# A two-layer hybrid block in split fp32: rotary projections and five gates turned, attention in steps, a last half chunk in two banks

## The chip, the cores and the metric

The kernel runs on one core of one Trainium2 chip. TensorE (PE) multiplies, VectorE (DVE), ScalarE (ACT) and GpSimd (POOL) work on what lies in SBUF and PSUM, SyncE (SP) starts transfers. The metric is device microseconds of one execution. The kernel before takes 939.03 us, the median of three runs (938.96 to 939.28).

## The reference, cut to what matters

Two layers over 256 tokens with 2048 channels, each of the form x + mix(norm(x) @ w_in) @ w_out. The even layer holds retention (8 heads, q and k rotated) and a selected attention of 8 heads; the odd layer a convolution over the sequence and an attention at three dilations. Every mixed part is multiplied by a gate, the silu of a projection of its own:

```python
def even_layer(x, ...):
    h = rms_norm(x, norm_g) @ w_in
    rq, rk, rv, rz, nq, kc, vc, ks, vs, kw, vw, ng, nz = split_cols(h, EVEN_SPLITS)
    o = retention_chunkwise(rotary(heads(rq), pos), rotary(heads(rk), pos), heads(rv))
    a_out = merge(rms_norm(o, ret_g)) * silu(rz)
    b_out = nsa_attention(nq, kc, vc, ks, vs, kw, vw, ng, ...) * silu(nz)
    return x + concat([a_out, b_out]) @ w_out

def odd_layer(x, ...):
    cu, cg, cz, dq, dk, dv, dz = split_cols(rms_norm(x, norm_g) @ w_in, ODD_SPLITS)
    c_out = conformer_conv(cu, cg, ...) * silu(cz)      # 1024 wide
    d_out = dilated_attention(dq, dk, dv, ...) * silu(dz)   # 512 wide
    return x + concat([c_out, d_out]) @ w_out
```

## The kernel before

All the large products are made in three passes of a short fp32 format (fp32r). A weight piece of 512 KB (`raw`, 128 rows x two k x 512 columns) is fetched by SP; ACT casts it to `wh` (line 109) and DVE subtracts, `wl = raw - wh` (line 110). The inputs are split likewise into `xh` and `xl`, one block of 512 channels each. A projection of 512 columns goes over four blocks (chunks) of channels, two pieces each. It has two forms in `project`:

- The normal form (lines 145 to 147): 128 tokens are the stationary operand and 512 weight columns stream. Tokens stand in the partitions of the result; two banks `mm0`, `mm1` of PSUM hold the two halves of the tokens.
- The flipped form (lines 139 to 141), used for the four rotary projections: 128 weight columns are stationary, 256 tokens stream, three products. Columns stand in the partitions, so that a head is turned as rotary needs it.

The gates are projected in the normal form: ACT takes them from PSUM with silu and the token's factor (line 708). Three in the odd layer and two in the even layer multiply a result that has channels in the partitions, so PE first transposes `z` in 8 pieces of 128x128 (`gated`, `turn`, line 315).

The weight pieces have five buffers (tag `raw`, `wh`, `wl`), and the projections three banks of PSUM (tag `mm`), which go round: the third projection half after a given one takes its bank. Two more banks hold scores (`sc`), two serve transposes (`tr`), one holds sums (`o`).

The order of instructions on each engine is not written out by hand. A scheduler with a simulated timeline sets it from the order in the code and from priorities (`tc.high_priority(offset=HPO)`); work of the attention is handed in as `pieces`, placed behind given weight chunks through `extra`/`take`. Every engine then runs its own list in order and waits at semaphores.

Names in the stages that matter here. Even layer: `pcs`, `pc`, `pch`/`pcl` are compressed scores and their split, `pst` (line 538) holds copies of them, `p`, `sm`, `nm` belong to a head's softmax (line 560 makes its maximum), `pTh`/`pTl` are its turned split. `rot` and `rT` are the rotated parts of q or k (lines 640 to 644), `rrow` (line 235) the row of token factors, `pb` the constants it is multiplied into. Odd layer: `acc` is the convolution's result, `chsum`/`csq`/`lnm`/`lnr`/`lnrow` its normalisation, `dsc`, `dp`, `dnm`, `dpT`, `dpo`, `do` the dilated attention's scores, weights, factors, turned weights, sums and results. `ACT_TABLE_LOAD` comes where ACT goes from one kind of function to another (silu, exp, square root).

At the start two projections share the first input blocks (`project_both`, lines 272 to 274: `mm` and `both`), and the squares of each block for its norm are taken behind the block's first projection (`square_block`, `sqb`, `sqs`). At the end the last half of the last projection is added to `xtok` in two parts of 256 columns (line 965), each with its own transfer to the output.

## Time and profile before

| | |
|---|---|
| profiled execution, whole | 939.11 us |
| its span, first to last instruction | 937.3 us |
| granted TensorE clock, mean | 0.999 |
| PE busy | 930.5 us (99%), 4949 matmuls |
| DVE busy | 642.3 us (69%) |
| ACT busy | 507.5 us (54%) |
| POOL busy | 71.1 us (8%) |
| DMA | 173.48 MB, mean 185 GB/s |

The profiled execution takes 1.8 us more than its span, and lies 0.08 us above the median of the runs. Busy time of PE is made of modelled ends, so that matmuls overlap in the rows; what one costs is read from the distance of the starts. Idle time of an engine matters only where PE waits for it.

### The profile page before, as it was taken

What the parts mean: (1) busy time and instruction counts of PE and PEld (TensorE: products, weight loads), DVE (VectorE), ACT (ScalarE), POOL (GpSimd) and SP (SyncE); (2) the same over time, 40 slices, a digit from 0 to 9 for tenths busy, and PEclk for the clock granted to TensorE, in tenths of its full rate; (3) what the DMA queues carried; (4) which work ended last, traced back from release to release, by engine and by line L of the source; (5) the groups of instructions that cost most, each with busy time, mean ns of one, the idle gap of its engine ahead of it and who ended that gap; (6) DMA issues with size and microseconds to landing.
All of it is one profiled execution on the core that took longest, in us unless ns stands there. A gap on an engine that the chain in (4) does not pass through costs nothing.

```text
span 937.3 us, 13151 instructions
## 1 busy us (share of the span) xinstructions
PE 930.5 (99%) x4949; PEld 798.7 (85%) x4949; DVE 642.3 (69%) x947; ACT 507.5 (54%) x762; POOL 71.1 (8%) x72
## 2 busy tenths in 40 slices
PE   8999999999999999999999999999999999999998
PEld 7889989989998888888888888888888888888886
DVE  7687657875654564654464499999999998546552
ACT  7566656655544544544465353556665444797341
POOL 0111100320220100000000000000000002200000
PEclk9999999999999999999999999999999999999999
DMA  9967754354446555555555555555555656434461
GB/s 332 348 204 220 249 189 149 120 176 156 152 164 207 161 170 182 185 195 181 196 185 168 192 180 180 190 190 190 185 186 185 202 197 189 148 116 157 149 226 53
DMA packets 52512, 173.48 MB, mean 185 GB/s; under 512 B 5728, under 2 KB 10720, under 8 KB 52320
## 3 DMA queue, kind: packets, MB, share of 16 engines
q1 hardware_dynamic: 52304, 172.63, 55.8%
q8 instruction: 39, 0.64, 0.3%
q14 instruction: 25, 0.20, 0.1%
q10 hardware_dynamic: 144, 0.01, 0.0%
HBM read 170.52 MB, written 2.10 MB: 184 GB/s over the span
## 4 chain that ended last, share of the span: by engine, by line
PE 97%; DMA 1%; DVE 1%; ACT 0%; issue 0%; SPq 0%; DVEq 0%
PE mm L145 25%; PE mm L147 25%; PE mm L146 25%; PE mm L139 3%; PE mm L141 3%; PE mm L140 3%; PE tr L315 3%; DMA raw<-in_ew 1%; PE dpo L931 1%; PE dsc L911 1%; PE cmph L377 1%; PE tr L579 1%; PE both L273 1%; PE both L274 0%; PE both L272 0%; PE mm L274 0%
## 5 line engine op out<-in xcount | busy, mean ns | idle before, releaser
L110 DVE TENSOR_TENSOR wl<-raw,wh 128x1024 fp32r<-128x1024 f32 (+2 forms) x322 | 385.1, 1202 | 215.0 <-ACT wh L109 208.1
L109 ACT CAST wh<-raw 128x1024 fp32r<-128x1024 f32 (+2 forms) x322 | 328.4, 1025 | 343.5 <-PE mm L147 252.1
L146 PE MATMUL mm<-wl,xh 128*128 128x512 f32 (+1 forms) x1056 | 406.4, 385 | 0.0
L145 PE MATMUL mm<-wh,xh 128*128 128x512 f32 (+1 forms) x1056 | 406.1, 386 | 0.0
L147 PE MATMUL mm<-wh,xl 128*128 128x512 f32 (+1 forms) x1056 | 403.3, 384 | 0.0
L147 PEld LDWEIGHTS mm<-wh,xl 128*128 128x128 f32 x1056 | 198.4, 188 | 38.1
L145 PEld LDWEIGHTS mm<-wh,xh 128*128 128x128 f32 x1056 | 198.2, 188 | 37.9 <-issue 0.2
L146 PEld LDWEIGHTS mm<-wl,xh 128*128 128x128 f32 x1056 | 198.5, 188 | 37.4
L801 DVE SCALAR_TENSOR_TENSOR cps<-apad,pb,cps 128x256 f32<-128x256 f32 x240 | 116.8, 487 | 5.3
L139 PE MATMUL mm<-xh,wh 128*128 128x256 f32 x256 | 73.2, 287 | 0.0
L140 PE MATMUL mm<-xh,wl 128*128 128x256 f32 x256 | 72.8, 285 | 0.0
L141 PE MATMUL mm<-xl,wh 128*128 128x256 f32 x256 | 72.5, 283 | 0.0
L140 PEld LDWEIGHTS mm<-xh,wl 128*128 128x128 f32 x256 | 49.0, 192 | 0.0
L141 PEld LDWEIGHTS mm<-xl,wh 128*128 128x128 f32 x256 | 49.0, 191 | 0.0
L139 PEld LDWEIGHTS mm<-xh,wh 128*128 128x128 f32 x256 | 48.9, 191 | 0.0
L567 ACT ACTIVATE p<-p,nm 128x128 f32<-128x128 f32 (+1 forms) x32 | 14.2, 445 | 15.5 <-DVE nm L563 15.4
L643 POOL TENSOR_TENSOR rot<-rot,pb 128x512 f32<-128x512 f32 x8 | 11.2, 1406 | 78.3 <-ACT rot L641 78.0
L299 ACT ACTIVATE sq<-d 128x128 f32<-128x128 f32 x48 | 14.3, 303 | 0.3
L273 PE MATMUL both<-wl,xh 128*128 128x512 f32 x32 | 12.8, 401 | 1.2 <-DVE wl L110 1.2
L644 POOL TENSOR_TENSOR rT<-rT,rot 128x512 f32<-128x512 f32 x8 | 13.1, 1660 | 0.0
L272 PE MATMUL both<-wh,xh 128*128 128x512 f32 x32 | 12.6, 394 | 0.0
L274 PE MATMUL both<-wh,xl 128*128 128x512 f32 x32 | 12.5, 390 | 0.0
(294 smaller groups left out, 724.0 us busy)
## 6 DMA issues: line engine op xcount, KB each, us to landing
raw<-in_ow SPq DMA_DIRECT2D x128, 512.0 KB, 4.5
raw<-in_ew SPq DMA_DIRECT2D x110, 512.0 KB, 4.2
raw<-in_ewo SPq DMA_DIRECT2D x32, 512.0 KB, 4.0
raw<-in_owo SPq DMA_DIRECT2D x24, 512.0 KB, 4.1
raw<-in_ewn SPq DMA_DIRECT2D x16, 268.0 KB, 3.5
xtok<-in_xtok SPq DMA_DIRECT2D x1, 2048.0 KB, 8.3
raw<-in_w1k SPq DMA_DIRECT2D x4, 512.0 KB, 6.4
raw<-in_w1v SPq DMA_DIRECT2D x4, 512.0 KB, 4.2
```

Source lines behind the costliest of these rows:

```text
L109: nc.scalar.copy(wh[:, k, :n], r)
L110: nc.vector.tensor_sub(wl[:, k, :n], r, wh[:, k, :n].bitcast(F32))
L139: nc.tensor.matmul(o, wh[:, k, cs], xh[:, kk, :], start=first and j == 0, stop=False, **kw)
L140: nc.tensor.matmul(o, wl[:, k, cs], xh[:, kk, :], start=False, stop=False, **kw)
L141: nc.tensor.matmul(o, wh[:, k, cs], xl[:, kk, :], start=False, stop=last, **kw)
L145: nc.tensor.matmul(o, xh[:, kk, ts], wh[:, k, :n], start=first, stop=False)
L146: nc.tensor.matmul(o, xh[:, kk, ts], wl[:, k, :n], start=False, stop=False)
L147: nc.tensor.matmul(o, xl[:, kk, ts], wh[:, k, :n], start=False, stop=last)
L273: nc.tensor.matmul(o, xh[:, kk, ts], wl[:, k, :], start=False, stop=False)
L299: nc.scalar.activation(sqv[:, t, h, :], view[:, t, h, :], AF.Square, accum_out=ss[:, t * nh + h:t * nh + h + 1])
L315: nc.tensor.transpose(pt[:, i * 128:(i + 1) * 128], b, ident)
L801: nc.vector.scalar_tensor_tensor(p, src, w, p, op0=ALU.mult, op1=ALU.add)
```

## The change

- The rotary projections and five gates (two even, three odd) go through `project_turned`: blocks of 256 columns, 128 weight columns stationary. `xh` and `xl` of a block now lie in one tile `xx`, so that one product of `wh` with both (2x256 columns streamed) and one of `wl` with `xh` (256 columns) take the place of three. The result stands in two halves of the bank, which are added on the way out.
- `evac_rotary` works per head: ACT copies one half to `rx` (two buffers), DVE adds the other, ACT makes two rotated copies, DVE and POOL multiply and add as before.
- A turned gate leaves PSUM by an ACT copy, a DVE add, a DVE product with the row of token factors (`rrow`, and a new `rrow2` for the odd layer) and a silu on ACT, for each 128 columns. Its transposes go; the product with the result is a plain DVE product (`done`).
- The pieces of the selected attention are cut into scores, turning and sums, ten in all; those of retention into scores and sums.
- The squares of the first three input blocks wait for the second projection's last piece of that block (`late`).
- The last half chunk of the last projection goes into two banks: 12 products of 256 columns in place of 6 of 512; the first 256 columns leave together with the sum so far of the other 256.
- `pst` is filled by 12 copies of 512 columns in place of 24 of 256.

```diff
+EV_TURNED = [(512 * h + 1024 * i + 256 * j, 512 * h + 1024 * i + 256 * j + 256)
+             for h in range(2) for i in range(2) for j in range(2)]
+EV_TURNED += [(6680 + 256 * j, 6936 + 256 * j) for j in range(4)]
...
+    def project_turned(src, lhs, evac, extra=None):
+        nch = src.shape[0]
+        acc = [ps.tile([128, 512], F32, name=f"mm{t}", tag="mm", bufs=MMB) for t in range(2)]
+        for c in range(nch):
+            with tc.high_priority(offset=HPO):
+                raw, wh, wl = (wp.tile([128, 2, 512], d, name=n, tag=n).rearrange("p a (b n) -> p (a b) n", n=256)
+                               for n, d in (("raw", F32), ("wh", F32R), ("wl", F32R)))
+                nc.sync.dma_start(raw, src[c])
+                nc.scalar.copy(wh, raw)
+                nc.vector.tensor_sub(wl, raw, wh.bitcast(F32))
+            xh, _, both = lhs[c]
+            for t in range(2):
+                cs = slice(t * 128, t * 128 + 128)
+                for k in range(4):
+                    last = c == nch - 1 and k == 3
+                    kw = dict(skip_group_check=True)
+                    nc.tensor.matmul(acc[t], wh[:, k, cs], both[:, :, k, :], start=c == 0 and k == 0, stop=False, **kw)
+                    nc.tensor.matmul(acc[t][:, :S], wl[:, k, cs], xh[:, k, :], start=False, stop=last, **kw)
+                if last:
+                    with tc.high_priority(offset=HPO):
+                        evac(t, acc[t])
...
+                    if tail and t == 1 and c == nch - 1 and hf == 1:
+                        end = ps.tile([128, 512], F32, name="mm2", tag="mm", bufs=MMB)
+                        for j, o in enumerate((acc[t][:, :256], end[:, :256])):
+                            js = slice(256 * j, 256 * j + 256)
+                            for k in range(2):
+                                kk, kw = 2 * hf + k, dict(skip_group_check=True)
+                                nc.tensor.matmul(o, xh[:, kk, ts], wh[:, k, js], start=j == 1 and k == 0, stop=j == 0, **kw)
+                                nc.tensor.matmul(o, xh[:, kk, ts], wl[:, k, js], start=False, stop=j == 0, **kw)
+                                nc.tensor.matmul(o, xl[:, kk, ts], wh[:, k, js], start=False, stop=j == 0 or k == 1, **kw)
+                            with tc.high_priority(offset=HPO):
+                                tail(j, acc[t], end)
+                        continue
...
+    def square_block(b, after=None):
         if b == 0:
             sqs[0] = hp.tile([128, S], F32, name="sqs", tag="h")
         sq = hp.tile([128, 4, S], F32, name="sqb", tag="h")
-        nc.scalar.activation(sq, xT[:, 4 * b:4 * b + 4, :], AF.Square)
+        nc.scalar.activation(sq, xT[:, 4 * b:4 * b + 4, :], AF.Square, bias=0.0 if after is None else after)
         nc.vector.tensor_add(sq[:, 0:2, :], sq[:, 0:2, :], sq[:, 2:4, :])
...
-                if q == 0 and c < nch - 1:
-                    square_block(c)
+                if q == 1 and c < nch - 1:
+                    nc.gpsimd.tensor_copy(late[:, c:c + 1], parts[1][1][:, 1, 511:512].bitcast(F32))
+                    nc.gpsimd.memset(late[:, c:c + 1], 0.0)
+                    square_block(c, late[:, c:c + 1])
...
-    pst = [hp.tile([128, 4, 2, 128], F32R, name=f"pst{g}", tag="h") for g in range(2)]
-    for h in range(8):
-        g, r = h // 4, slice(32 * (h % 4), 32 * (h % 4) + 32)
+    pst = [hp.tile([128, 2, 4, 128], F32R, name=f"pst{g}", tag="h") for g in range(2)]
+    for j in range(4):
         for n, src in enumerate((pch, pch, pcl)):
-            v = src[r].rearrange("p (t g) k -> p t g k", t=2)[:, :, g, :]
-            (nc.vector.tensor_copy if n else nc.scalar.copy)(pst[g][32 * n:32 * n + 32, h % 4], v)
+            (nc.vector.tensor_copy if n else nc.scalar.copy)(pst[j // 2][32 * n:32 * n + 32, j % 2], src[32 * j:32 * j + 32])
...
+    def nsa_piece(m):
+            if m > 2 and m % 2:
+                nsa_sum(m - 2)
+            if 0 < m < 9:
+                if m % 2:
+                    for n in ("h", "l"):
+                        npt[n] = pp.tile([128, 6, 2, 128], F32R, name="pT" + n, tag="pT")
+                nsa_turn(m - 1, nsp.pop(m - 1), npt["h"], npt["l"])
+            if m < 8:
+                nsp[m] = nsa_scores(m)
+    pieces = [nsa_piece(m) for m in range(10)]
...
-        def f(b, p):
-            hs = slice(2 * b, 2 * b + 2)
-            pv = p.rearrange("p (h s) -> p h s", h=2)
-            cb, sb = (x.unsqueeze(1).to_broadcast([128, 2, S]) for x in (cosR, sinR))
-            nc.scalar.copy(rot[0:64, hs, :], pv[64:128])
-            nc.scalar.copy(rot[64:128, hs, :], pv[0:64])
-            nc.vector.tensor_tensor(T[:, hs, :], pv, cb, op=ALU.mult)
-            nc.gpsimd.tensor_tensor(rot[:, hs, :], rot[:, hs, :], sb, op=ALU.mult)
-            nc.gpsimd.tensor_add(T[:, hs, :], T[:, hs, :], rot[:, hs, :])
+        def f(h, p):
+            x = sp.tile([128, S], F32, name="rx", tag="rx", bufs=2)
+            nc.scalar.copy(x, p[:, S:])
+            nc.vector.tensor_add(x, p[:, :S], x)
+            nc.scalar.copy(rot[0:64, h, :], x[64:128])
+            nc.scalar.copy(rot[64:128, h, :], x[0:64])
+            nc.vector.tensor_mul(T[:, h, :], x, cosR)
+            nc.gpsimd.tensor_mul(rot[:, h, :], rot[:, h, :], sinR)
+            nc.gpsimd.tensor_add(T[:, h, :], T[:, h, :], rot[:, h, :])
...
-            project(ew[4 + 3 * hf + i], 512, lhs, evac_rotary(T), extra=take((1,3)), flip=True)
+            f = evac_rotary(T)
+            for j in range(2):
+                project_turned(a["ewt"][4 * hf + 2 * i + j], lhs, lambda t, p: f(2 * j + t, p), extra=take((3,)))
...
-        pieces += [ret_piece(hf, h, qk[0], qk[1], v, dm, gr, hold) for h in range(4)]
...
+        pieces += [together(pieces.pop(), scores[0]) if hf else scores[0]]
+        pieces += [together(sums[h - 1], scores[h]) for h in range(1, 4)] + [sums[3]]
...
-        project(src, 512, lhs, lambda t, p: nc.scalar.activation(z[:, t, :], p, AF.Silu, scale=r[:, t:t + 1]),
-                extra=extra)
-
-        def turn():
-                pt = transpose4([z[:, t, (2 * j + k) * 128:(2 * j + k + 1) * 128] for k in range(2) for t in range(2)])
-                with tc.high_priority(offset=HPO):
-                    d = dst[:, hs, :].rearrange("p a b -> p (a b)")
-                    nc.vector.tensor_mul(d, pt, d)
-                    split(xh[:, hs, :], xl[:, hs, :], dst[:, hs, :])
...
+    def gated(srcs, dst, row, turn, n=4):
+        z = hp.tile([128, 4, S], F32, name="z", tag="h")
+        xh, xl, xx = block_pair()
+        for j in range(2):
+            def evac(t, p, j=j):
+                v = z[:, 2 * j + t, :]
+                nc.scalar.copy(v, p[:, S:])
+                nc.vector.tensor_add(v, p[:, :S], v)
+                nc.vector.tensor_mul(v, v, row)
+                nc.scalar.activation(v, v, AF.Silu)
+            project_turned(srcs[j], lhs, evac, extra=first(turn if j == 0 else None, take((1, 3))))
+        def done():
+                nc.vector.tensor_mul(dst[:, hs, :], dst[:, hs, :], z[:, hs, :])
+                split(xh[:, hs, :], xl[:, hs, :], dst[:, hs, :])
...
+    rrow2 = token_row(rstd2, "rrow2")
...
-        extra = take(range(4))
-        if i == 2:
-            extra = {c: extra.get(c, []) + ([turns[c]] if c < 2 else []) for c in range(4)}
-        block, turn = gated(ow[13 + i], (acc[0], acc[1], do)[i], rstd2, extra)
+        turn = (lambda: [f() for f in turns]) if i == 2 else None
+        block, done = gated(a["owt"][2 * i:2 * i + 2], (acc[0], acc[1], do)[i], rrow2, turn)
         mix.append(block)
-        turns.append(turn)
+        turns.append(done)
...
-            w = 256 if n == 3 and t else 512
-            for c in range(0, 512, w):
-                k = 512 * n + c
-                v = xtok[:, t, k:k + w]
-                nc.vector.tensor_add(v, p[:, c:c + w], v)
-                nc.sync.dma_start(out[t, :, k:k + w], v)
+            v = xtok[:, t, 512 * n:512 * n + 512]
+            nc.vector.tensor_add(v, p, v)
+            nc.sync.dma_start(out[t, :, 512 * n:512 * n + 512], v)
         return f
+    def evac_tail(j, p, end):
+        v = xtok[:, 1, D - 512:]
+        if j == 0:
+            nc.vector.tensor_add(v, p, v)
+            nc.sync.dma_start(out[1, :, D - 512:D - 256], v[:, :256])
+        else:
+            nc.vector.tensor_add(v[:, 256:], end[:, :256], v[:, 256:])
+            nc.sync.dma_start(out[1, :, D - 256:], v[:, 256:])
```

How the order changes is seen best at three places.

VectorE in the even layer, where the compressed scores have been split and the first rotary projection leaves PSUM; before, the two halves of the projection (`mm0_1567`, `mm1_1568`) are read by the product for `rT`:

```order
L538 COPY pst0_1530<-pcl_1522 32x256 x4
L538 COPY pst1_1531<-pcl_1522 32x256 x4
L560 ISA p_1867,nm_1866<-sc_1859,pm_518 128x2x128
L560 ISA nm_1866 128x1
L560 ISA p_1867,nm_1866<-sc_1859,pm_518 128x128
L560 ISA nm_1866 128x1
L560 ISA p_1867,nm_1866<-sc_1859,pm_518 128x2x128
L560 ISA nm_1866 128x1
L110 TENSOR_TENSOR wl_2083<-raw_2081,wh_2082 128x1024
L460 TENSOR_TENSOR pTl_1691<-tr_1717,pTh_1690 128x4x128
L563 TENSOR_SCALAR nm_1866<-nm_1866 128x4
L642 TENSOR_TENSOR rT0_0_1565<-mm0_1567,pb_521 128x512
```

VectorE at the same place of the changed kernel; `rx_1640` and `rx_1656` are the first two heads, already out of PSUM, and `mm0_1689` is the bank of the third:

```order
L596 ISA p_1817,nm_1816<-sc_1809,pm_521 128x2x128
L596 ISA nm_1816 128x1
L574 COPY pst0_1533<-pcl_1525 32x512 x2
L574 COPY pst1_1534<-pcl_1525 32x512 x2
L690 TENSOR_TENSOR rT0_0_1556<-rx_1640,pb_524 128x256
L690 TENSOR_TENSOR rT0_0_1556<-rx_1656,pb_524 128x256
L599 TENSOR_SCALAR nm_1816<-nm_1816 128x4
L498 TENSOR_TENSOR pTl_1796<-tr_1797,pTh_1795 128x4x128
L498 TENSOR_TENSOR pTl_1796<-tr_1804,pTh_1795 128x2x128
L687 TENSOR_TENSOR rx_1771<-mm0_1689,rx_1771 128x256
```

The third head's bank is now read behind the copies of `pst`, the products of the first two heads and `pTl`.

ScalarE in the odd layer before, at the first gate (`z_7125`) and in the stretch behind it:

```order
L862 ACTIVATE csq_7263<-acc1_5405 128x1024
L708 ACT_TABLE_LOAD
L708 ACTIVATE z_7125<-mm0_7128,rstd2_4726 128x512
L708 ACTIVATE z_7125<-mm1_7129,rstd2_4726 128x512
L919 ACT_TABLE_LOAD
L919 ACTIVATE dp_7337,dnm_7336<-dp_7337,dnm_7336 128x384
L921 ACTIVATE dp_7337<-dp_7337,dnm_7336 128x384
L919 ACTIVATE dp_7398,dnm_7397<-dp_7398,dnm_7397 128x768
```

ScalarE in the changed kernel, from the row of the convolution's normalisation to the second gate's copies out of PSUM:

```order
L269 COPY lnrow_7220<-tr_7218 128x256
L994 COPY dpT_7296<-tr_7297 128x384
L943 ACT_TABLE_LOAD
L943 ACTIVATE acc0_4947<-acc0_4947,pb_524 128x256 x4
L994 COPY dpT_7364<-tr_7365 128x512
L943 ACTIVATE acc1_5304<-acc1_5304,pb_524 128x256 x4
L985 ACT_TABLE_LOAD
L985 ACTIVATE dp_7440,dnm_7439<-dp_7440,dnm_7439 128x384
L985 ACTIVATE dp_7506,dnm_7505<-dp_7506,dnm_7505 128x768
L1008 COPY do_7023<-dpo_7284 128x256
L774 COPY z_7305<-mm0_7307 128x256
L774 COPY z_7305<-mm1_7308 128x256
```

The gate's banks `mm0_7307` and `mm1_7308` are read behind the convolution's silus, two table loads and two exponentials.

ScalarE a little later before: the weights `dp_7588` of one unit of the dilated attention, with what stands ahead of them:

```order
L928 COPY dpT_7470<-tr_7471 128x384
L928 COPY dpT_7526<-tr_7527 128x512
L919 ACT_TABLE_LOAD
L919 ACTIVATE dp_7588,dnm_7587<-dp_7588,dnm_7587 128x384
L921 ACTIVATE dp_7588<-dp_7588,dnm_7587 128x384
```

ScalarE in the changed kernel at a unit of that size (also named `dp_7588`):

```order
L994 COPY dpT_7446<-tr_7447 128x384
L168 CAST wh_7715<-raw_7714 128x1024
L994 COPY dpT_7512<-tr_7513 128x512
L985 ACT_TABLE_LOAD
L985 ACTIVATE dp_7588,dnm_7587<-dp_7588,dnm_7587 128x384
L168 CAST wh_7768<-raw_7767 128x1024
L774 COPY z_7305<-mm1_7456 128x256
L987 ACTIVATE dp_7588<-dp_7588,dnm_7587 128x384
```

Between the two exponential steps of the unit there are now a weight cast and a copy of the gate.

## Rows read from the trace of the kernel before

**Rows 1.** The page, busy time of each engine.
```profile
PE 930.5 (99%) x4949; PEld 798.7 (85%) x4949; DVE 642.3 (69%) x947; ACT 507.5 (54%) x762; POOL 71.1 (8%) x72
```
**Rows 2.** Windows: length, then PE, PEld, DVE, ACT, POOL, clock, DMA.
```profile
160.00:250.00 90.00, 90.00 (x649) 84.98 (x648) 64.87 (x159) 54.78 (x112) 16.18 (x13) 1.00 0.47 156
...
790.00:890.00 100.00, 100.00 (x523) 85.29 (x522) 56.28 (x84) 66.99 (x94) 11.33 (x7) 1.00 0.45 147
```
**Rows 3.** Chain of waits, 741 to 764: start, time, line.
```profile
741.28 0.45 PE mm L147 x2
...
763.04 0.45 PE mm L147 x2
```
**Rows 4.** Chain of waits, 249.5 to 251.
```profile
250.12 0.24 PE mm L139 x2
```
**Rows 5.** Timeline of PE: start, time, instruction, idle before.
```profile
142.60 1.04 PE L315 MATMUL tr<-pa,nq 128*128 128x128 f32 x8
143.39 0.36 PE L140 MATMUL mm<-xh,wl 128*128 128x256 f32 x1
```
**Rows 6.** Groups of PE instructions by line.
```profile
L315 PE MATMUL tr<-pa,z 128*128 128x128 f32 x40 | 5.8, 272 | 0.0
```
**Rows 7.** Timeline of PE at the start.
```profile
11.34 0.50 PE L272 MATMUL both<-wh,xh 128*128 128x512 f32 x1
12.71 0.50 PE L273 MATMUL both<-wl,xh 128*128 128x512 f32 x1 [0.87 <-DVE wl L110]
...
26.49 0.61 PE L272 MATMUL mm<-wh,xh 128*128 128x512 f32 x2
27.40 0.50 PE L273 MATMUL both<-wl,xh 128*128 128x512 f32 x1 [0.30 <-DVE wl L110]
```
**Rows 8.** Timeline of DVE at the start.
```profile
11.10 0.42 DVE L204 TENSOR_TENSOR sqs<-sqb 128x256 f32<-128x256 f32 x1
11.44 2.35 DVE L110 TENSOR_TENSOR wl<-raw,wh 128x1024 fp32r<-128x1024 f32 x2
```
**Rows 9.** Timeline of DVE at the end.
```profile
933.53 0.76 DVE L965 TENSOR_TENSOR xtok<-mm,xtok 128x256 f32<-128x256 f32 x2 [0.67 <-PE mm L147]
```
**Rows 10.** Timeline of PE in the even layer.
```profile
158.03 0.60 PE L315 MATMUL tr<-pa,pc 128*128 128x128 f32 x4
```
**Rows 11.** Timeline of DVE, 160 to 172.
```profile
160.56 0.68 DVE L460 TENSOR_TENSOR pcl<-tr,pch 128x512 fp32r<-128x512 f32 x1
161.28 2.37 DVE L538 CAST pst<-pch 32x256 fp32r<-32x256 f32 x8
...
166.38 0.42 DVE L560 CUSTOM_DVE_ANT_0 p<-sc,pm 128x256 f32<-128x256 f32 x1
...
171.21 0.41 DVE L460 TENSOR_TENSOR pTl<-tr,pTh 128x256 fp32r<-128x256 f32 x1
```
**Rows 12.** Timeline of ACT, 803 to 835.
```profile
803.68 1.28 ACT L708 ACT_TABLE_LOAD   x1
804.98 1.27 ACT L708 ACTIVATE z<-mm,rstd 128x512 f32<-128x512 f32 x2
...
809.57 0.94 ACT L919 ACTIVATE dp<-dp,dnm 128x768 f32<-128x768 f32 x1 [0.46 <-DVE dnm L918]
...
820.24 0.37 ACT L235 COPY lnrow<-tr 128x256 f32<-128x256 f32 x1 [1.65 <-PE tr L233]
820.57 0.48 ACT L928 COPY dpT<-tr 128x384 f32<-128x384 f32 x1
821.04 1.05 ACT L109 CAST wh<-raw 128x1024 fp32r<-128x1024 f32 x1
...
823.40 3.55 ACT L877 ACTIVATE acc<-acc,pb 128x256 f32<-128x256 f32 x7
...
829.71 0.61 ACT L919 ACTIVATE dp<-dp,dnm 128x384 f32<-128x384 f32 x1
...
830.33 0.57 ACT L928 COPY dpT<-tr 128x512 f32<-128x512 f32 x1
```

More of the change, by code (lines that the diff above doesn't have):

```diff
@@ L55 @@
            (3072, 3584), (4608, 5120), (3584, 4096), (5120, 5632), (4096, 4608), (5632, 6144),
-           (6144, 6656), (6656, 7168), (7168, 7680), (2048, 2560), (2560, 3072), (7680, 8192)]
+           (6144, 6656), (6656, 7168), (7168, 7680)]
+OD_TURNED = [(2048 + 256 * j, 2304 + 256 * j) for j in range(4)] + [(7680, 7936), (7936, 8192)]
 @with_exitstack
@@ L112, in prep, with project @@
         return parts
-    def project(src, n, lhs, evac, korder=None, lazy=None, extra=None, cut=None,
-                flip=False):
+    def project(src, n, lhs, evac, extra=None, tail=None):
         nch = src.shape[0]
         acc = [ps.tile([128, 512], F32, name=f"mm{t}", tag="mm", bufs=MMB) for t in range(2)]
-        order = korder or list(range(nch))
-        for i, c in enumerate(order):
-            if lazy:
-                lazy(c)
-            parts = prep(src[c], n, cut=(lambda k: cut(c, k)) if cut and i < 3 else None)
-            xh, xl = lhs[c]
+        for c in range(nch):
+            parts = prep(src[c], n)
+            xh, xl, _ = lhs[c]
             for hf in range(2):
@@ new lines, in project @@
+                    for k in range(2):
+                        kk = 2 * hf + k
+                        last = c == nch - 1 and kk == (1 if tail and t else 3)
+                        nc.tensor.matmul(o, xh[:, kk, ts], wh[:, k, :n], start=c == 0 and kk == 0, stop=False)
+                        nc.tensor.matmul(o, xh[:, kk, ts], wl[:, k, :n], start=False, stop=False)
+                        nc.tensor.matmul(o, xl[:, kk, ts], wh[:, k, :n], start=False, stop=last)
+                    if last and hf:
@@ L248, in project_both @@
         nch = srcs[0].shape[0]
+        late = const.tile([128, 4], F32, name="late")
         for c in range(nch):
@@ L574, in nsa_head, with nsa_turn @@
                 nc.vector.tensor_scalar(cut(p, b)[t], cut(p, b)[t], sm[:, 2 * t + b:2 * t + b + 1], None, op0=ALU.mult)
+        return p
+    def nsa_turn(h, p, pTh, pTl):
+        e = h % 2
         for c0, blocks in ((2, (0, 1, 2, 3)), (0, (4, 5))):
@@ L673, in ret_piece, with together, f @@
         return f
+    def together(*fs):
+        def f():
+            for g in fs:
+                g()
+        return f
     for hf in range(2):
@@ L686, in hybrid_kernel @@
         nc.sync.dma_start(gr, row_bcast(a["retg"][hf * 512:hf * 512 + 512], 512))
-        hold = [None]
-        pieces += [ret_piece(hf, h, qk[0], qk[1], v, dm, gr, hold) for h in range(4)]
+        rh = {}
+        scores = [ret_scores(h, qk[0], qk[1], dm, rh) for h in range(4)]
+        sums = [ret_sum(hf, h, v, gr, rh) for h in range(4)]
+        pieces += [together(pieces.pop(), scores[0]) if hf else scores[0]]
+        pieces += [together(sums[h - 1], scores[h]) for h in range(1, 4)] + [sums[3]]
     def mix_block(src):
-        xh = xtp.tile([128, 4, S], F32R, name="xh", tag="xh")
-        xl = xtp.tile([128, 4, S], F32R, name="xl", tag="xl")
+        xh, xl, xx = block_pair()
         for j in range(2):
@@ L726, in hybrid_kernel @@
     for i in range(2):
-        block, turn = gated(ew[10 + i], no[i], rstd[0], first(turn, take(range(4))))
+        block, turn = gated(a["ewt"][8 + 2 * i:10 + 2 * i], no[i], rrow, turn)
         mix.append(block)
@@ L734, in evac_z @@
             nc.vector.tensor_mul(o[:, t, :], o[:, t, :], z[:, t, :])
-        project(ew[12 + i], 512, lhs, evac_z, extra=first(turn, take(range(4))))
+        project(ew[6 + i], 512, lhs, evac_z, extra=first(turn, take(range(4))))
         turn = lambda i=i: mix.append(mix_block(ros[i]))
```

101 lines of the change are left out of this document (42 added, 59 removed).

## The prediction

> **What bounds the kernel now.** I read the page's busy times first: PE is busy for 99% of the span, no other engine for 70% [rows 1]. The windows then say whether that holds where the change works: in the stage of the selected attention and the rotary projections PE is busy for 90.00 of 90 us, in the stage of the odd gates for 100.00 of 100, at full clock; DVE and ACT have a quarter to half of those stretches free [rows 2]. So every product that PE loses is won, and every wait of PE is lost, since there is none now. Busy time of PE overlaps, so I take its prices from distances between starts in the chain of waits: a projection in the normal form is 96 products (4 blocks, 2 pieces, 2 halves, 2 k, 3 passes) and takes 763.04 - 741.28 = 21.76 us, 0.2267 us for 512 columns [rows 3]; 256 columns take 0.24 / 2 = 0.120 us [rows 4]; eight transposes with the change of kind behind them about 0.88, 0.11 each [rows 5]. Only the start has gaps on PE: 12.71 - 11.34 - 0.23 = 1.14 us and 27.40 - 26.49 - 0.45 = 0.46 us, both until a `wl` of DVE [rows 7].
>
> **What PE does.** A rotary projection of 512 columns is 4 x 4 x 4 x 3 = 192 products of 256 columns, 23.04 us. Turned it is 64 of 512 and 64 of 256: 14.51 + 7.68 = 22.19 us. Four of them: -3.4 us. A gate is 21.76 + 8 x 0.11 = 22.64 us with its transposes, of which the five gates have 40 [rows 6]; turned 22.19: five times -0.45, -2.2 us. The tail's last half chunk goes from 6 x 0.2267 to 12 x 0.120, +0.1; the additional row `rrow2` is one f32 product of 256 columns in two passes, about 0.4. Sum: -5.1 us.
>
> A product with 512 columns that lie in two separate runs of 256 is not in the trace. From below it costs 0.2267, like one run; from above 0.240, like two products. I take 0.2267, for the columns are as many; with 0.240, 576 products give 7.7 us back, and PE wins nothing.
>
> On this the Trainium skill speaks against the change: in "TensorE: Matmul & The Clock Gate", section "Step-by-step: what each phase is for", a stream of products costs its columns alone. By that one product of 512 is worth two of 256, the rotary projections win nothing, and the sum would be 3.4 us higher. The trace does not agree, since two of 256 take 0.240 and one of 512 takes 0.2267.
>
> **The start.** The `wl` for which PE waits at 12.71 begins at 11.44, right behind the sum of squares `sqs`, 0.42 us [rows 8]; with the squares of the first three blocks behind the second projection's last piece, this work on ACT and DVE no longer stands ahead of the first `wl`. The two gaps hold 1.6 us. At best they go whole, at worst the transfer of the weights is what comes last and 0.4 goes. I take -1.4. The squares come later in their turn, but the token factors that need them are asked for only after eight more pieces.
>
> **The end.** Behind the last product two additions of 256 columns take 0.76 us [rows 9]; now the first runs under the last six products and one of 0.42 is left. -0.35.
>
> **The pst copies, the pieces, the extra work on ACT and DVE.** Between 160 and 250 us DVE has 25 us free and ACT 35 [rows 2]; the additional reads of half a bank (0.41 each [rows 11]) are hidden by PE's products, as long as no bank comes free too late. There the cover fails in three places.
>
> **First wait: the fourth rotary block.** Its first product `mm1_1837` needs the bank of `mm0_1689`, freed by DVE's addition for the third head. I count both sides from the four transposes of `pc` (0.44 us, ending at 158.47 in the trace [rows 10]). PE has 31 products of `mm_1836` (16 x 0.2267 + 15 x 0.120 = 5.4), two heads' scores (each three of 512 and three of 256, 1.04), the row's two passes (0.4) and six transposes (0.66): 8.6 us. DVE ends `pcl` at 161.24, 2.8 behind the transposes [rows 11]. Then it has eight copies of `pst`, which were sixteen in 4.7 us: between 2.4 (as many ns each as before) and 4.7 (twice), taken at 0.49 each by the ratio of `pcl` (512 columns, 0.68) to half of `pTl` (256, 0.41), 3.9 in all; four maxima of at most 0.42, two of them half as wide, 1.3; two products for `rT`, 0.8; `nm` 0.1; `pTl` 0.68 + 0.41; the addition 0.41 [rows 11]. That is 2.8 + 7.6 = 10.4 us. PE waits 1.8; with the hand-overs between ACT and DVE on the way I take +2.2, between 0 and 4.5. Behind it on PE stands everything.
>
> **Second wait: the second gate's second half.** `mm1_7456` needs the bank of `mm0_7307`. On ACT the copy of that bank stands behind the row `lnrow` of the convolution's normalisation, which PE makes. From the end of that product PE has 6.7 us of work until `mm1_7456`: ten products of `mm_7455`, nine transposes of `dp`, nine of `dpo` (0.11 each) and six score products. ACT has `lnrow` 0.37, `dpT` 0.48, a table load 1.28, eight silus at 3.55 / 7 = 0.507, `dpT` 0.57, a table load 1.28, exponentials 0.61 and 0.94, `do` and the copy of `z` at 0.37 (the size of `lnrow`): 10.3 us [rows 12], and DVE's addition 0.41. PE waits 10.7 - 6.7 = 4.0 us, between 2 and 5.5.
>
> In the trace an instruction follows a table load 1.30 us after its start [rows 12]. The Trainium skill, "ScalarE: Activation LUTs", section "What ACT_TABLE_LOAD costs", gives the same 1.283 us and adds a drain of 1.38 to every switch. By that the two loads of this chain would cost 2.8 us more; the trace shows no drain, so the sum stays.
>
> **Third wait: one unit of the dilated attention.** The transposes of `dp_7588` come 11.4 us after PE resumes. From the copy of `mm0_7307` ACT has two more copies (0.37), two `dp` (0.61, 0.94), a load, three silus (0.507), four weight casts (1.05), two `dpT` (0.48, 0.57), a load, the exponential 0.61, a copy and the product 0.61: 13.2 us, of which 0.4 runs before PE resumes. +1.3, between 0 and 2.5.
>
> **The sum.** 939.1 (the profiled execution, 0.1 from the median) - 5.1 - 1.4 - 0.35 + 2.2 + 4.0 + 1.3 = 939.8 us. No change that a measurement of this kernel can tell (0.2%, 1.9 us, is about its limit).
>
> **Rivals.**
> *The waits don't come.* ACT and DVE reach the banks in time, and what PE loses is won whole: 939.1 - 6.9 = 932.2, or about 935 with the third head's wait alone. For it speaks that before no wait of PE is left in either stage [rows 2], that my chains give each instruction its full length though neighbours overlap by some 0.1, and that the order of ACT is the scheduler's answer to the same load. Against it, the chain of ACT would have to be shorter by 4 us of 10.3, and two table loads are 2.6 of it. Chance 0.26.
> *ScalarE stays behind in the odd gates (slower).* It has 33 us free in these 100 [rows 2]. The turned gates bring eight more table loads (10.3 us), twelve copies (4.4) and twelve silus of 256 in place of six of 512 (0.507 against 0.63, 2.3): 17 us, half of what is free, and most of it inside 40 us. If ACT is still late when the second gate is through, the first half of the third gate's banks waits like the second's: another 4.0, and with the rotary wait at its upper end 939.8 + 4.0 + 2.3 = 946; with one of them 942 to 944. It decides itself at the copy of `mm0_7605`: it comes true if that copy starts after PE is ready for the first product of `mm1_7766`, the half that takes its bank. Chance 0.25.
> *Two runs of columns cost as two products.* 939.8 + 7.7 = 947.5. For it speaks only that no row shows such an input, against it that the columns are as many. Chance 0.05.
>
> **How the numbers follow.** The forecast, 939.8, has 0.44; its own range is 937 to 942. Within it 0.36 lie less than 0.2% from 939.0 (937.1 to 940.9), 0.07 above and 0.01 below. The first rival gives 0.26 to faster, the other two 0.30 to slower. So faster 0.27, same 0.36, slower 0.37. The range for 8 in 10 reaches from 933.5, which leaves out the better half of the first rival's cases, to 945.5, which leaves out the third and the worst of the second.
>
> **What would show it.** In the profile after, the count of PE should fall from 4949 by some 130; a rotary projection of 256 columns should take 11.1 us from first to last start where nothing stands between; PE should show idle time before the first product of `mm1` at about 165 us, with DVE as the releaser, and 4 us of it near 820, with DVE's addition for `z` behind ACT's copies. PE's gap at 11 us should be gone. If the stretch between 790 and 890 shows no idle PE, the second and third waits were wrong, and the time is below 936; if the distance of starts of the 512 column products is over 0.235, the price of the turned product was.

## The result and the profile after

The changed kernel takes 945.38 us (median of four runs, 943.29 to 945.99) against 939.00 for the kernel before on the same chip: a ratio of 1.0063, interval 1.0050 to 1.0076. It is slower by 0.6%, where I had forecast no change (939.8) with 0.37 for slower; the time lies 0.1 us inside the range.

The profiled execution took 945.79 us, its span is 944.0. On the page, busy time has hardly moved [rows 1]:

```profile
PE 931.6 (99%) x4821; PEld 794.0 (84%) x4821; DVE 665.9 (71%) x1005; ACT 533.6 (57%) x829; POOL 74.3 (8%) x94
```

TensorE (PE) has 128 products fewer, about as forecast. The windows of the two stages say more (length, PE, PEld, DVE, ACT, POOL, granted clock, DMA); before, PE was busy for 90.00 and 100.00 us there at full clock [rows 2]:

```profile
160.00:250.00 90.00, 86.41 (x483) 75.49 (x482) 67.70 (x163) 58.75 (x127) 20.01 (x22) 0.96 0.48 155
790.00:890.00 100.00, 96.33 (x565) 84.57 (x564) 67.84 (x109) 82.05 (x122) 10.78 (x7) 0.98 0.44 141
```

Each stage has lost some 3.6 us to idle time, and in each the clock is under 1.00. The list of waits of PE (engine, line, releaser: us in total, times, longest) puts both on one wait each:

```profile
PE mm L176 <- DVE z L775: 3.6, 1, 3.6
PE mm L176 <- DVE rx L687: 3.6, 1, 3.6
PE cold L195 <- DVE heat L192: 1.0, 1, 1.0
PE both L308 <- DVE wl L116: 0.8, 1, 0.8
```

The first is the second gate's second half (my second wait), the second the fourth rotary block (my first). A third wait isn't there. The timeline of PE shows what the list doesn't, the products behind the first of them:

```profile
171.92 0.79 PE L176 MATMUL mm<-xx,wh 128*128 128x512 f32 x1 [3.59 <-DVE rx L687]
172.51 0.41 PE L177 MATMUL mm<-xx,wl 128*128 128x256 f32 x1
172.72 0.63 PE L176 MATMUL mm<-xx,wh 128*128 128x512 f32 x1
173.36 0.63 PE L176 MATMUL mm<-xx,wh 128*128 128x512 f32 x1
...
178.42 0.40 PE L176 MATMUL mm<-xx,wh 128*128 128x512 f32 x1
178.77 0.40 PE L176 MATMUL mm<-xx,wh 128*128 128x512 f32 x1
```

Two products of 512 columns in a row (with one of 256 between) start 0.64 us apart at 173 and 0.35 apart at 178. Narrow windows over the two places, the granted clock in the column before the last two:

```profile
170.00:171.00 1.00, 0.00 (x0) 0.00 (x0) 1.00 (x2) 0.81 (x4) 1.00 (x2) 0.87 0.00 0
171.00:177.00 6.00, 5.08 (x16) 4.31 (x17) 5.96 (x21) 5.45 (x19) 3.30 (x5) 0.50 0.00 0
...
833.00:836.00 3.00, 2.69 (x8) 2.31 (x9) 1.91 (x6) 2.97 (x6) 0.00 (x0) 0.50 0.00 0
```

Towards the end of each wait the granted clock fell to 0.50 (1.2 of 2.4 GHz), and it stayed there for 6 to 7 us at the first place and some 3 us at the second, through products that waited for nothing. The four runs follow it: at a mean clock of 0.998 it is 943.29 us, at 0.994 it is 945.99; so how long the clock stays down differs from one execution to the next.

At the end and at the start the rows that answer to [rows 9] and [rows 7]:

```profile
939.89 0.69 DVE L1034 TENSOR_TENSOR xtok<-mm,xtok 128x512 f32<-128x512 f32 x1
940.68 0.42 DVE L1037 TENSOR_TENSOR xtok<-mm,xtok 128x256 f32<-128x256 f32 x1
```

```profile
11.44 0.47 PE L307 MATMUL both<-wh,xx 128*128 128x512 f32 x1
12.66 0.50 PE L308 MATMUL both<-wl,xx 128*128 128x512 f32 x1 [0.76 <-DVE wl L116]
```

The tail does what was forecast. At the start the gap near 27 us is gone, the one near 12 us has stayed.

### The profile page after: what moved, and what is told of

Read it like the earlier page. It is cut to its first block, busy times and chain, and to the rows that moved or that the text cites. A ratio compares the mean times of both kernels' runs of the same rounds, so it can differ in the third digit from the quotient of the medians.

```text
span 944.0 us, 13054 instructions
## 1 busy us (share of the span) xinstructions
PE 931.6 (99%) x4821; PEld 794.0 (84%) x4821; DVE 665.9 (71%) x1005; ACT 533.6 (57%) x829; POOL 74.3 (8%) x94
## 4 chain that ended last, share of the span: by engine, by line
PE 96%; DVE 2%; ACT 1%; DMA 1%; SPq 0%; issue 0%; DVEq 0%
PE mm L149 21%; PE mm L151 21%; PE mm L150 21%; PE mm L176 14%; PE mm L177 7%; PE tr L353 2%; PE cmph L415 1%; PE both L308 1%; PE both L309 1%; PE both L307 1%; PE dpo L997 1%; PE dsc L977 1%; DMA raw<-in_ew 1%; PE mm L309 1%; PE mm L308 1%; PE mm L307 1%
## 5 line engine op out<-in xcount | busy, mean ns | idle before, releaser
L116 DVE TENSOR_TENSOR wl<-raw,wh 128x1024 fp32r<-128x1024 f32 (+2 forms) x250 | 294.3, 1183 | 157.1 <-ACT wh L115 150.0
L150 PE MATMUL mm<-wl,xx 128*128 128x512 f32 (+1 forms) x894 | 341.8, 383 | 0.0
L149 PE MATMUL mm<-wh,xx 128*128 128x512 f32 (+1 forms) x894 | 341.5, 384 | 0.0
L151 PE MATMUL mm<-wh,xx 128*128 128x512 f32 (+1 forms) x894 | 339.9, 383 | 0.0
L176 PE MATMUL mm<-xx,wh 128*128 128x512 f32 x576 | 209.5, 405 | 7.2 <-DVE z L775 3.6
L151 PEld LDWEIGHTS mm<-wh,xx 128*128 128x128 f32 x894 | 168.0, 188 | 32.0
L150 PEld LDWEIGHTS mm<-wl,xx 128*128 128x128 f32 x894 | 168.0, 188 | 31.9
L149 PEld LDWEIGHTS mm<-wh,xx 128*128 128x128 f32 x894 | 167.7, 188 | 31.8 <-issue 0.2
L177 PE MATMUL mm<-xx,wl 128*128 128x256 f32 x576 | 163.2, 285 | 0.0
L176 PEld LDWEIGHTS mm<-xx,wh 128*128 128x128 f32 x576 | 109.8, 191 | 31.9 <-DVE z L775 3.8
L169 DVE TENSOR_TENSOR wl<-raw,wh 128x1024 fp32r<-128x1024 f32 x72 | 89.4, 1244 | 52.3 <-ACT wh L168 52.0
L177 PEld LDWEIGHTS mm<-xx,wl 128*128 128x128 f32 x576 | 110.7, 192 | 0.6
## 6 DMA issues: line engine op xcount, KB each, us to landing
xtok<-in_xtok SPq DMA_DIRECT2D x1, 2048.0 KB, 10.6
```

The source lines that it names most:

```text
L116: nc.vector.tensor_sub(wl[:, k, :n], r, wh[:, k, :n].bitcast(F32))
L149: nc.tensor.matmul(o, xh[:, kk, ts], wh[:, k, :n], start=c == 0 and kk == 0, stop=False)
L150: nc.tensor.matmul(o, xh[:, kk, ts], wl[:, k, :n], start=False, stop=False)
L151: nc.tensor.matmul(o, xl[:, kk, ts], wh[:, k, :n], start=False, stop=last)
L169: nc.vector.tensor_sub(wl, raw, wh.bitcast(F32))
L176: nc.tensor.matmul(acc[t], wh[:, k, cs], both[:, :, k, :], start=c == 0 and k == 0, stop=False, **kw)
```

## The experiments

Ten kernels ran, in three sets, each set beside the kernel before (938.91, 939.73 and 939.32 us, the medians of each set). My theory at this point: the loss is the two waits for a bank, and the clock that falls in them; the products won less than forecast. The rivals: the loss is in the turned products themselves (the two runs of columns), or in the load on ScalarE as a whole.

### Four rx tiles: the first wait alone

```diff
-            x = sp.tile([128, S], F32, name="rx", tag="rx", bufs=2)
+            x = sp.tile([128, S], F32, name="rx", tag="rx", bufs=4)
```

> The changed kernel with four buffers `rx` in place of two, nothing else. Theory: in the changed kernel the ACT copy of the third head's bank waits for the buffer that the first head gives back only after its product with cos, and that waits for `rrow`; so PE stands 3.75 us at 168 us and then runs some 5 us at half its clock (2.6 us). With four buffers the third and fourth head leave PSUM before the `pst` copies, and both go: 945.4 - 6.3 = about 939 us, no idle time of PE near 168 and clock 1.00 between 160 and 250. Rival: it is the load of DVE (copies of `pst`, POOL beside it) that makes the bank late, and the wait only moves to the next bank: 943 us or more.

941.72 us, ratio 1.0029 (1.0018 to 1.0040): neither the 939 of the theory nor the 943 of its rival. The wait for `rx` is gone and the clock is 1.00 from 160 to 250. A smaller wait has come in its place; the list of waits:

```profile
PE mm L176 <- DVE z L775: 3.6, 1, 3.6
PE tr L619 <- DVE p L610: 1.4, 1, 1.4
```

What freed the bank late was therefore the chain ScalarE's copy to `rx` hung on. With two tiles the copy for the third head had to wait until VectorE had read the first head's tile, behind the copies of `pst`; ScalarE's row in the changed kernel:

```profile
169.75 0.71 ACT L686 COPY rx<-mm 128x256 f32<-128x256 f32 x2 [1.80 <-DVE rT L690]
```

Of 6.2 us (3.6 idle, 2.6 of half clock) 1.4 came back as the new wait, and PE waited 0.5 and 0.3 us more at the start of this profile. The spans differ by 4.1 us, the medians by 3.7.

### The gate leaves its bank through a tile of its own: the second wait alone

```diff
-                nc.scalar.copy(v, p[:, S:])
-                nc.vector.tensor_add(v, p[:, :S], v)
-                nc.vector.tensor_mul(v, v, row)
+                x = sp.tile([128, S], F32, name="zx", tag="zx", bufs=2)
+                nc.scalar.copy(x, p[:, S:])
+                nc.vector.tensor_add(x, p[:, :S], x)
+                nc.vector.tensor_mul(v, x, row)
```

> The changed kernel, but a turned gate goes out of PSUM through a small tile of its own (`zx`, 256 columns, two buffers) and only the product with the row writes `z`; the same number of instructions. Theory: the second gate's copy out of PSUM stands late on ACT because `z` takes the buffer of the convolution's mean, not because ACT lacks time; with a tile of its own it comes ahead of `lnrow`, the wait of 3.8 us at 830 goes and with it the half clock behind it (1.4 us): about 940 us. Rival (ACT is too full between 790 and 840, with eight more table loads): the wait stays within 1 us of its size or moves to the third gate: 943 to 946 us.

942.89 us, 1.0039 (1.0024 to 1.0054). The wait for `z` is gone and the clock is 1.00 from 790 to 890; two short ones (1.1 and 0.7 us) on the dilated attention's `dp` and `dpT` stand in its place, so that the time fell by 2.5 us and not by the 5.2 of the theory. The copy to `z` read a bank that had long been ready. Into a small tile of its own it starts at 818 us, ahead of `lnrow` at 822; into `z` it started at 832:

```profile
818.34 0.35 ACT L775 COPY zx<-mm 128x256 f32<-128x256 f32 x1
```

So the copy's target set its place in ScalarE's order. `z` is a large tile and shares its buffers with tiles of the convolution; that it was the mean's buffer for which it stood late is my reading, and no row shows it.

### Both

The two edits together, the gates through the four `rx` tiles.

> Both together: four buffers `rx`, which the turned gates use too on their way out of PSUM. Theory: no wait of PE is left behind the first 30 us: 945.4 - 6.3 - 5.2 = about 934 us, faster than the kernel before by some 5 us. Rival (the turned products themselves cost more than they save): 939 us or more.

936.92 us, 0.9977 (0.9968 to 0.9987): faster than before by 0.23%, and than the changed kernel by 0.85%, though 3 us short of the 934 that I expected. Its page, its windows and its largest wait inside the layers:

```profile
PE 927.4 (99%) x4821; PEld 790.1 (84%) x4821; DVE 665.4 (71%) x1005; ACT 526.4 (56%) x825; POOL 74.8 (8%) x94
160.00:250.00 90.00, 88.59 (x512) 77.47 (x511) 70.84 (x177) 60.26 (x134) 23.44 (x26) 1.00 0.48 161
790.00:890.00 100.00, 99.44 (x579) 87.10 (x578) 67.31 (x106) 75.07 (x115) 10.79 (x7) 1.00 0.45 145
```

```profile
PE tr L619 <- DVE p L610: 1.4, 1, 1.4
```

The two waits and what hangs on them are worth 8 us, more than the whole loss of 6.4; the turned products themselves aren't the loss. ScalarE's load as a whole isn't the cause of either wait: each went in a run of its own in which ScalarE was as busy (532.2 and 533.2 us, 21 table loads) as in the changed kernel (533.6). Here it has less to do, 526.4 us with 17 table loads, because the order came out another way. Alone the edits won 3.7 and 2.5 us, together 8.5; how much of the 2.3 us between is owed to the four loads was not tried. The wait of 1.4 us leaves the clock at 1.00, the waits of 3.6 did not.

### Products without use inside the first wait

```diff
+        if h == 0:
+            warm2 = const.tile([128, 128], BF16, name="warm2")
+            nc.scalar.copy(warm2, pTh[:, 0, e, :].bitcast(F32))
+            spare = ps.tile([128, 512], F32, name="spare", tag="o")
+            for _ in range(36):
+                nc.tensor.matmul(spare[:, :128], warm2, heat, start=True, stop=True)
```

> The changed kernel with 36 products of 128 bf16 columns (3.8 us) put on PE exactly into its wait at 168 us; their operand is a small copy made on ACT when the transposes ahead of the wait are done, and their result is not used. Theory: the bank comes free as late as before, so the wait costs the same 3.75 us, but PE does not idle and its clock stays at 1.00 behind it; the 2.6 us go: the profiled execution some 2.6 us under the changed kernel's 945.8, about 943 us. Rival (the half clock comes from something else, the load of the turned products for one): no change, 945 us with a clock of 0.5 behind 172.

946.41 us, 1.0077. A miss: the copy came late too, and PE was idle for 3.05 us ahead of these products:

```profile
171.34 2.86 PE L626 MATMUL spare<-heat,warm 128*128 128x128 bf16 x36 [3.05 <-ACT warm L623]
```

```profile
172.00:173.00 1.00, 1.00 (x19) 1.00 (x17) 1.00 (x8) 0.98 (x5) 0.00 (x0) 0.82 0.00 0
173.00:176.00 3.00, 3.00 (x18) 2.71 (x16) 2.96 (x10) 2.93 (x12) 2.42 (x4) 0.50 0.00 0
```

It shows one thing: the clock fell between 172 and 173, when PE had been busy again since 171.34. It comes late, and products issued behind the idle time didn't prevent it. Whether the idle time is its cause was left to the next one.

### Work without use ahead of the first wait

```diff
+            if h == 0 and c0 == 0:
+                spare = ps.tile([128, 512], F32, name="spare", tag="o")
+                for _ in range(34):
+                    nc.tensor.transpose(spare[:, :128], p[:, :128], ident)
```

> The changed kernel with 34 transposes of 128 columns without use (about 0.11 us each, 3.7 in all) put into TensorE's order ahead of the wait for the bank of the third rotary head, so that the engine arrives at that bank just when it comes free: the bank comes no earlier, but TensorE isn't idle before it. Theory (the half clock follows the idle time, and costs by itself some 2.6 us): no idle time over 1 us before that product, granted clock 1.00 from 165 to 180, and the time falls by 2 to 3 us from the changed kernel's 945.4, to 942 to 943.5; the second wait stays as it is. Rival (the half clock comes from what the engines do in that stretch, not from the idle time): the clock falls to 0.50 at 171 as before, and the time stays at 945 to 946. A second rival (work in the wait is dear, it delays other things): 946 or more with full clock.

943.90 us, 1.0046 (1.0033 to 1.0058). Four transposes of `pc` stand at the head of the chain that frees the bank; from their first start to the waiting product it is 12.8 us in both kernels (161.5 to 174.30 here, 159.1 to 171.92 in the changed one), and VectorE's addition that frees the bank starts 12.3 us behind them in both, so the bank comes no earlier in the chain. But PE isn't idle, and the clock holds:

```profile
168.00:170.00 2.00, 2.00 (x21) 2.00 (x20) 1.94 (x7) 0.95 (x2) 1.92 (x3) 1.00 0.00 0
170.00:172.00 2.00, 2.00 (x16) 1.86 (x15) 1.96 (x4) 0.00 (x1) 1.29 (x2) 1.00 0.00 0
172.00:178.00 6.00, 6.00 (x35) 5.14 (x34) 5.93 (x17) 4.59 (x16) 3.64 (x5) 1.00 0.00 0
```

So the half clock is the idle time's doing, not that of the instructions in this stretch: 3.7 us of work for nothing, and the kernel isn't slower for it. The time is 1.5 us less, where I expected 2 to 3; the two intervals overlap, so that size is not shown by the times. The rows give it: eight products and their partners at 0.64 in place of 0.35 us are 2.3, and with the edges 2.6. The profiled execution, 946.06 us, is even as long as the changed kernel's (945.79); the other four took 943.54 to 944.12. In its first 20 us, where the changed kernel's clock is 1.00, there is another stretch at 0.50, from 14.6 to 18.0:

```profile
0.00:20.00 20.00, 17.04 (x85) 13.36 (x86) 11.82 (x20) 13.11 (x20) 2.13 (x11) 0.91 0.90 318
```

It stands behind two waits of 1.1 and 0.8 us close together, so a shorter wait can be followed by the half clock too.

### Both parts of the input in one run

```diff
-        x = xtp.tile([128, 2, 4, S], F32R, name="xx", tag="xx")
-        return x[:, 0], x[:, 1], x
+        x = xtp.tile([128, 4, 2, S], F32R, name="xx", tag="xx")
+        return x[:, :, 0, :], x[:, :, 1, :], x
```

> The kernel without the two waits (four rx tiles, the gates leave their bank through them too; it took 936.9), with both parts of the input laid side by side, so that a product's 512 columns are one run and not two runs of 256. If the two runs are what makes the pair of a turned product 0.350 us and not 0.2267 + 0.120 = 0.3467: 576 pairs x 0.0033 = 1.9 us less, 935, and a pair of 0.347 in the trace. If the price is that of a stationary half of 128 columns at a stride, or of the switch between a product of 512 and one of 256: no change, 936.5 to 937.3, pair 0.350.

937.28 us, 0.9972 (0.9961 to 0.9983), the same as with two runs (0.9977), and so are its products:

```profile
L176 PE MATMUL mm<-xx,wh 128*128 128x512 f32 x576 | 206.4, 401 | 0.1
L177 PE MATMUL mm<-xx,wl 128*128 128x256 f32 x576 | 161.7, 282 | 0.0
```

With two runs the rows read 206.3, 401 and 161.7, 282. A pair costs 0.350 us (mean of the 489 undisturbed pairs of the changed kernel), not 0.2267 + 0.120 = 0.3467, but the two runs are not why. What is, stays open; in the starts the surplus lies on the product of 512 columns, which is 0.2335 us ahead of a product of 256 and 0.227 ahead of another of 512.

### The rotary's sums on VectorE

```diff
-            nc.gpsimd.tensor_mul(rot[:, h, :], rot[:, h, :], sinR)
-            nc.gpsimd.tensor_add(T[:, h, :], T[:, h, :], rot[:, h, :])
+            nc.vector.tensor_mul(rot[:, h, :], rot[:, h, :], sinR)
+            nc.vector.tensor_add(T[:, h, :], T[:, h, :], rot[:, h, :])
```

> The kernel without the two waits, with the rotary's last product and addition (32 instructions of 256 columns) on VectorE and not on GpSimd. Theory (VectorE's instructions between two SBUF tiles take about twice their time while GpSimd works): the first rotary product takes 0.42 us a head also around 170 (0.76 with GpSimd beside it), the weights' second parts 1.2 (1.69), the copies of pst 0.42 throughout; GpSimd idle there. VectorE gets 32 x 0.42 = 13 us of work, spread over 150 us in which it has a quarter free, so the time stays within 1 us of 936.9, the lower if the remaining wait of 1.4 us for the weights p goes. Rival (those instructions are long for another reason, their place or their operands): the same lengths of 0.76 and 1.69 with GpSimd idle, and the time is up by 1 to 4 us by the added work on VectorE.

935.84 us, 0.9956 (0.9943 to 0.9968), the fastest of all. VectorE's timeline with GpSimd beside it (the kernel with both edits):

```profile
169.59 3.05 DVE L690 TENSOR_TENSOR rT<-rx,pb 128x256 f32<-128x256 f32 x4
172.56 3.45 DVE L169 TENSOR_TENSOR wl<-raw,wh 128x1024 fp32r<-128x1024 f32 x2
```

and without:

```profile
170.13 1.42 DVE L690 TENSOR_TENSOR rT<-rx,pb 128x256 f32<-128x256 f32 x4
171.47 1.21 DVE L169 TENSOR_TENSOR wl<-raw,wh 128x1024 fp32r<-128x1024 f32 x1
```

Four products take 1.42 us rather than 3.05, a weights' second part 1.21 rather than 1.7. The work was slow because GpSimd worked, and the wait of 1.4 us for `p` is gone. VectorE's 32 additional instructions cost nothing that shows. One expectation failed: the second four copies of `pst` still take 2.23 us. GpSimd has two instructions left there (168.56 to 170.19), and the last of the four, beside them, takes 0.93 us, the other three 0.42 each.

### The odd gates as before

The three odd gates in the normal form with their transposes, on the kernel with both edits.

> The kernel without the two waits, with the three gates of the odd layer in the form of before (products of 512 columns with the input stationary, eight transposes each, silu from the bank, no row rrow2), the rotary projections and the two even gates turned. By the price that I predicted with (turned gate 22.19, normal 22.64): 3 x 0.45 - 0.4 = 1.0 us more than 936.9, 937.9. By the pair measured since, 0.350 (64 x 0.350 = 22.40): 3 x 0.24 - 0.4 = 0.3 more, 937.2, which is no difference that can be told. Rival (the turned gates cost in waits of ScalarE's table loads, which the trace hides): it gets faster, 935 to 936.

937.23 us, 0.9973 (0.9964 to 0.9982), where the turned gates gave 0.9977. Turning the odd gates wins and costs nothing that can be told, once the wait is away; by the pair's price it should be 0.3 us.

### The rotary projections as before

192 products of 256 columns a projection, on the kernel with both edits.

> The kernel without the two waits (four rx tiles, the gates through them; it took 936.9), with the rotary projections in the form of before (192 products of 256 columns a projection of 512, each bank read whole, sums on GpSimd in 512 columns), the gates turned as in the change. By the pair measured since (64 x 0.350 = 22.40 for a turned projection, 192 x 0.120 = 23.04 for the old one): 4 x 0.64 = 2.6 us more, less up to 1.4 if the wait that is left for the weights p goes with it: 938.1 to 939.5. By the price that I predicted with (22.19): 4 x 0.85 = 3.4 more, 938.9 to 940.3. Rival (the turned rotary gains nothing, the gain of that kernel over before is in its start and its end): 936 to 937.

938.42 us, 0.9988 (0.9979 to 0.9997), inside the lower band. Against 0.9977 with the turned rotary that is 1.0 us (1.5 by the two times), and the intervals overlap. The trace says more, though its execution is the shortest of eleven (936.99 us): the spans are 935.2 and 935.1, but the 1.4 us for `p` and 0.8 at the start are not waited for here, so its products take 2.3 us longer, close to the 2.6 of the pair's price.

### Start and end alone

The kernel before with the late squares and the two banks of the last half chunk.

> The kernel before with two edits of the change alone: the squares of the first three blocks behind the second projection's last piece, and the last half chunk in two banks. Prediction's terms: start -1.4, six products in two pieces +0.1, end -0.35, 1.65 us in all. What the trace of the changed kernel showed: the gap of 0.3 to 0.5 at 27 us gone and about 1 us left in front of the second pass of the first piece, because the transfer of the weights comes last there; the end 0.5 shorter; so 0.7 + 0.5 - 0.1 = 1.1 us less than before. Both are near what can be told; the two gaps and the last 5 us of the trace are to show it.

938.76 us, 0.9990 (0.9981 to 0.9999): 0.6 us, less than either estimate. The end is as in the changed kernel. At the start of this profile PE waits twice near 12 us:

```profile
12.10 0.50 PE L311 MATMUL both<-wh,xh 128*128 128x512 f32 x1 [1.07 <-ACT wh L109]
13.36 0.50 PE L312 MATMUL both<-wl,xh 128*128 128x512 f32 x1 [0.76 <-DVE wl L110]
```

Behind `wh` stands the weights' transfer. In the changed kernel's chain of waits it is the step that comes last there:

```profile
4.47 5.81 DMA raw<-in_ew
...
10.30 1.06 ACT wh L115
```

It landed in time for 11.44 there and too late here. VectorE's squares were in front of `wl` before; now that they aren't, the transfer sets the start, and its arrival differs from run to run by about as much as the step was to win: the cast behind it starts between 9.67 and 11.13 us in the profiles of this change.

## Why the prediction was off

The two profiles, term by term (excess of the distances between starts over their usual size, in each stretch):

| term, us | predicted | measured |
|---|---|---|
| PE's work | -5.1 | -2.6 |
| gaps at the start | -1.4 | -0.7 |
| end | -0.35 | -0.45 |
| first wait | +2.2 | +3.7 |
| second wait | +4.0 | +3.8 |
| third wait | +1.3 | 0 |
| half clock behind the waits | not in the sum | +2.6 and +1.4 |
| scattered small gaps | 0 | -0.9 |
| sum | +0.7 | +6.8 |

That 945.38 us still lies in the range is luck: the range ends at 945.5, two of the four runs (945.79 and 945.99) are above it, and it reached so far because of rivals that didn't come true.

**What was right.** Both waits came, at the products, banks and releasers named. The second was sized within 0.2 us of idle time: from `lnrow` on ScalarE to the product it is 833.31 - 822.69 = 10.6 us in the trace, 10.7 in my chain, table loads included [rows 12]:

```profile
822.69 0.37 ACT L269 COPY lnrow<-tr 128x256 f32<-128x256 f32 x1 [2.82 <-PE tr L267]
...
823.51 1.28 ACT L943 ACT_TABLE_LOAD   x1
824.81 2.08 ACT L943 ACTIVATE acc<-acc,pb 128x256 f32<-128x256 f32 x4
...
829.35 1.28 ACT L985 ACT_TABLE_LOAD   x1
830.64 0.61 ACT L985 ACTIVATE dp<-dp,dnm 128x384 f32<-128x384 f32 x1
...
832.43 0.91 ACT L774 COPY z<-mm 128x256 f32<-128x256 f32 x3
```

The instruction behind a load starts 1.30 and 1.29 us after the load does, so that a load costs here what the sum gave it. The rival "the waits don't come" fell with this.

**The step that failed: a wait was priced at its idle time alone.** Every wait in the sum ends when the bank comes. The products behind it were taken at full price, and 4.0 us of the error of 6 is that they ran at half clock. On that the Trainium skill has a rule that I didn't weigh ("TensorE: Matmul & The Clock Gate", section "HAM oscillation — how this bites in real kernels": an engine that waits long enough is throttled, and starts the next work cold). The trace agrees: the clock is 0.50 behind 3.6 us of idle time, twice.

**The product's price.** Of the 2.5 us that PE's work won less, 1.9 are the pair: 0.350 for 0.3467, 576 times. I took the lower end, one run of 512; the upper, 0.240 for that product, would have been 7.7 us. The truth lies a quarter of the way up, and the reason that I gave for the upper end, the two runs, is refuted. The other 0.6 us I can't place; how the trace's distances are shared between this row and the scattered gaps depends on what is taken as usual, and the two rows together (-3.5) are near the -3.2 that the measured pair gives.

**The first wait, +3.7 for +2.2.** The chain of waits on VectorE:

```profile
163.18 0.42 DVE pst L574
...
166.60 0.86 DVE pst L574
167.47 0.87 DVE pst L574
168.35 0.85 DVE pst L574
169.24 0.76 DVE rT L690 x2
170.00 0.61 DVE nm L599
170.61 0.92 DVE pTl L498 x2
171.53 0.34 DVE rx L687
```

From `pcl`'s end to the bank it is 8.7 us, not 7.6. The eight copies take 4.7 us, my upper end, but not because they are twice as wide: the first four take 0.43 each and three of the others 0.86, with GpSimd at work. `nm`, four elements, takes 0.6 rather than 0.1. Ahead of that `pcl` ended 3.6 us behind the transposes of `pc`, not 2.8. PE's side was right: 168.17 - 159.59 = 8.6 us from these transposes to the bank, as counted.

**The start.** "At worst the transfer of the weights is what comes last" is what happened; I took a value near the best end.

**The third wait** was 1.3 us in my sum, counted from PE's resuming behind the second. There PE lost 1.4 us to the half clock, which by itself would cover it; this wasn't tried alone.

**The slower rival got the time but not the mechanism.** ScalarE recovers before the third gate: no product of that gate waits. 945 us lie in that rival's band for another reason.

## What to carry to other kernels

On an engine that is busy for 99% of the span, price a new wait of some us at its idle time and the half clock behind it: in the changed kernel's profile 3.6 us cost 5.2 to 6.3. Before products are moved, ask of each bank which small tile or buffer its reader hangs on; four small tiles and another place for one copy turned 0.63% slower into 0.23% faster. Take prices of VectorE's work between SBUF tiles from rows where GpSimd does what it will do then.

## What the runs showed of the hardware

In the profiles of the changed kernel and of the four runs with one or both of its waits left, the clock went to 0.50 at each of seven waits of 3.05 to 3.6 us, and stayed there for 3 to 7 us; at a wait of 1.4 to 1.5 us, in four runs, it didn't. How much of that stretch falls on products, and so its price, is not the same each time: 2.6 and 1.4 us in one execution. Shorter waits are not safe: behind the two of 1.1 and 0.8 us at the start the clock fell in one profile and not in two others with the same two waits. The kernel before has neither long wait, and still 12 of its 53 executions beside the experiments show a mean clock of 0.998, with a median of 940.8 us against 939.2 for the 34 at 1.000.

VectorE beside GpSimd: four products of two SBUF tiles took 3.05 us and not 1.42, a copy 0.86 and not 0.43, a difference of 1024 columns 1.7 and not 1.2. The Trainium skill ("Advanced Engine Details and Errata", section "GPSIMD Details") says that the two share an interface for reading and one for writing, and names as what collides the instructions with two SBUF inputs and those in a 2-port mode. The trace agrees for the products and differences, and adds the size, about twice. The copies have one SBUF input, and no row shows whether they ran in such a mode.
